# Samples' attention over the cached keys and values: steps of four tiles in place of two, and a fifth tile place

## The chip, the cores and the metric

The kernel runs on one core of one Trainium2 chip. The metric is device time in microseconds (us), the median of several runs. A core has five engines: TensorE (PE, matmuls; its weight loads are shown apart as PEld), VectorE (DVE), ScalarE (ACT), GpSimd (POOL) and SyncE (SP, which here only issues DMAs). Each takes its own instructions in order and waits on semaphores for the others. DMAs are issued by SP and POOL.

## What is computed

One layer of a decoder for two groups of tokens that share the weights: a prompt of 512 tokens, and 8 samples of 8 tokens each (64 in all). The layer is a mixer (two recurrences over one combined input projection), a cross-attention over 256 memory entries, and a gated feed-forward part, each between two norms and with a residual. All of it is float32. The change is in the cross-attention:

```python
qx = (u @ w_xq).reshape(bsz, length, 4, 256)
sc = einsum('blhd,bmhd->bhlm', qx, mem_k) * 256 ** -0.5
pr = softmax(sc, axis=-1)
o = einsum('bhlm,bmhd->blhd', pr, mem_v).reshape(bsz, length, 1024) @ w_xo
x = x + _rms(o) * g_post_x
```

For the prompt, `mem_k` and `mem_v` are computed in the kernel from `mem_prompt` with the weights `w_mem_k` and `w_mem_v`. For the samples they are inputs, `cache_mem_k` and `cache_mem_v`, of 8 samples x 256 entries x 4 heads x 256 values each, 8.4 MB a piece.

## The kernel before, in words

Activations lie transposed, channels on the 128 partitions and tokens along the free axis, prompt and samples side by side (576 columns, cut into halves of 256 and 320 or of 288). A float32 product with a weight is made of three faster ones: weight and activation are each split into a rounded high part and a low remainder, and PE does high by high, high by low and low by high (L202, L203, L205 in `gemm`; L795 to L797 for the memory's values). `split_w` (L175 to L187) loads a weight of 512 KB into one of two buffers called raw with a DMA on SP (L175), casts it on ACT to the high part whi (L180) and subtracts on DVE, or half on DVE and half on POOL, for the low part wlo (L187). whi and wlo have three buffers each. The weight's raw buffer is free when the low part is made, and its whi and wlo when PE has used them.

The instructions are written down in one order, and a scheduler with a timeline of its own then decides how the five engines' instructions interleave; `tc.issue_after` ties an instruction behind another one.

The attention of the prompt runs over the heads h = 3, 2, 1, 0 (the loop ahead of `attn_values(*last)`): query projection (`xq`, tile ps_xq), the memory's keys of the head (`mem_key`, ps_mk), transposes of the probabilities and attention times values of the head before (`attn_values`, ps_pt and ps_ov), scores and softmax (`attn_scores`, ps_at), the memory's values of the head (`mem_value`, ps_v). Behind the loop comes the output projection (`xo`, ps_xo), first for the tokens 0 to 287.

The attention of the samples is strewn into this as generators. `attn_samples_k(hb)` and `attn_samples_v(hb)` do scores with softmax, and probabilities times values, for the four samples 4 hb to 4 hb + 3. Both call `pick` (from L1395 on), which takes per sample two tiles of 128 x 1024 float32 (512 KB) out of the cache. `cached` (L1384 to L1389) loads such a tile with a DMA on SP (L1388) into the next of the places in `kv`, in turn: three in the slot s5 (the tiles called kva) and one in a pool of its own (kvb). For every tile PE does four matmuls of 32 columns (L1401), one for each head, into the 32 output partitions of that head; they are full float32 and show as two instructions each. When both samples of a pair are done, DVE takes from each head's rows those that belong to the sample (L1409, L1411). The pairs use two PSUM banks in turn (B0, B1). The softmax of the four samples and two transposes (ps_pts, L1427) end `attn_samples_k`; two transposes (ps_ots, L1436) and the split for the output projection end `attn_samples_v`.

The generators yield after the first sample of each pair and between the pairs, so that each takes four steps of two tiles: 16 steps in all. `sample_step(m)` takes the next step and ties it behind the instruction m. Steps are taken behind the first `xq` of a head, inside `mem_key`, inside `attn_scores` and behind `mem_value`; the last generator's four are taken in the loop of `xo` at j = 0, 1, 3 and 5. The order is: scores of the second four samples beside head 2, scores of the first four beside head 1, values of the second four beside head 0, values of the first four beside `xo`.

Ahead of all this, in the output projection of the mixer (ps_o, `out1` and `out2`), `presplit` (L1165 to L1183) prepares weights of later stages: it loads one on POOL's queue (tile prel, L1181), casts it on ACT (preh, L1174), subtracts on DVE (L1175) and writes the low part to DRAM on POOL's queue (pre, L1176). SP loads the memory's input (memraw, L1198) there, and further weights for ACT to cast (wmh, L191).

Of the kernel before, what the change touches and what calls it, by code (L numbers as in the profile page):

```python
# [11 lines left out]
F32 = mybir.dt.float32  # L12
# [7 lines left out]
P = 128  # L20
# [95 lines left out]
def build(nc, tc, ctx, I, O):  # L116
# [14 lines left out]
    def SL(slot, name, dt=F32, shape=(P, KT, T)):  # L131

        return big.tile(list(shape), dt, name=name, tag="s%d" % slot, bufs=1)


    def GP(name="g"):
        return pg.tile([P, 512], F32, name=name, tag="g")
# [17 lines left out]
    def C32(k):  # L155
        a, b = _c32[k]
        return c32[:, a:b] if b <= NLONG else c32e[:, a - NLONG:b - NLONG]
# [14 lines left out]
    def split_w(src, n=1024, cut=CUT, acc=False, pool=None, to=None, raw=None):  # L172
        if raw is None:
            raw = wp.tile([P, 1024], F32, name="raw", tag="raw", bufs=2)
        loads.append(S.dma_start(raw[:, :n], src))  # L175
        if to:
            split(*to, raw[:, :n])
            return to
        hi, lo = [(pool or wp).tile([P, 1024], F32R, name=k, tag=k, bufs=NWX if pool else 3) for k in ("whi", "wlo")]
        casts.append(A.copy(hi[:, :n], raw[:, :n]))  # L180
        for e, a, b in ((V, 0, cut), (G, cut, n)):
            if b > a and e is G and acc:

                A.activation(lo[:, a:b], hi[:, a:b].bitcast(F32), AF.Copy, scale=-1.0)  # L184
                G.dma_start(lo[:, a:b], src[:, a:b], accum_op=ALU.add)  # L185
            elif b > a:
                e.tensor_tensor(lo[:, a:b], raw[:, a:b], hi[:, a:b].bitcast(F32), op=ALU.subtract)  # L187
        return hi, lo

    def split(hi, lo, src, eng=None, cast=None):  # L190
        c = (cast or A.copy)(hi, src)  # L191
        (eng or V).tensor_tensor(lo, src, hi.bitcast(F32), op=ALU.subtract)  # L192
        return c

    def gemm(ps, units, xh, xl, t0, n, k0=0, k1=None, order=None, late=0):


        tiles = [(hi[:, j * P:(j + 1) * P], lo[:, j * P:(j + 1) * P]) for hi, lo, nk in units for j in range(nk)]
        order = order or range(len(tiles))
        for i, k in list(enumerate(order))[k0:k1]:  # L200
            (wh, wl), ah, al = tiles[k], xh(k, t0, n), xl(k, t0, n)
            mm(ps, wh, ah, start=i == 0, stop=False)  # L202
            mm(ps, wh, al, start=False, stop=False)  # L203
            for c in range(late) if i == late - 1 else [i] if i >= late else ():
                m = mm(ps, tiles[order[c]][1], xh(order[c], t0, n), start=False, stop=c == len(tiles) - 1)  # L205
        return m
# [503 lines left out]
    for g in range(2):  # L710
# [13 lines left out]
        for h in range(8):  # L724
            k, j = h % 2, (8 * g + h) // 2
# [434 lines left out]
    at = st.enter_context(tc.tile_pool(name="attn", bufs=1, reuse_waits="tile"))  # L1160
# [60 lines left out]
    def out2(j, i):  # L1221
        return gemm2([(*weights(("o", j), I["wout"][j, 1], cut=1024), KT)], act(mixm_h), act(mixm_l), o2_evac(j), "ps_o2", [i])
# [30 lines left out]
    m = out2(7, 0)  # L1253
    with tc.issue_after(m.ins):
        rc = rstd_cols([ssq], HCHUNKS[1], "po1", alloc=B0)
    m = out2(6, 0)
# [9 lines left out]
    s5 = SL(5, "kva", F32, (P, 4608))  # L1266
# [3 lines left out]
    def sample_step(m):  # L1270

        with tc.issue_after(m.ins):
            next(steps, None)

    def mem_act(i):
        return lambda k, t0, n: memh[:, i, k, t0:t0 + n]

    def mem_key(h, ws=None):

        mk = at.tile([P, 2, 2, 256], F32R, name="mk", tag="mk", bufs=1)  # L1280
        mo = at.tile([P, 2, 256], F32, name="mko", tag="mo", bufs=2)
        for kk in range(2):
            ps = GP("ps_mk")[:, 0:256]
            m = gemm(ps, [(*(ws[kk] if ws else split_w(I["wmk"][2 * h + kk])), KT)], mem_act(0), mem_act(1), 0, 256)
            if kk == 0:
                sample_step(m)
            V.tensor_tensor(mo[:, kk, :], ps, rmem_b, op=ALU.mult)
            split(mk[:, 0, kk, :], mk[:, 1, kk, :], mo[:, kk, :], None if ws else G)
        S.dma_start(O["mk"][:, 2 * h:2 * h + 2, :], mo)
        return (mk, m) if ws else mk  # L1290

    def mem_value(h, ws=None):

        mv = at.tile([P, 2, 2, 256], F32R, name="mv", tag="mv", bufs=1)
        mo = at.tile([P, 2, 256], F32, name="mvo", tag="mo", bufs=2)

        def ev(_, ps):
            for c in range(2):
                A.activation(mo[:, c, :], ps[:, c * 256:(c + 1) * 256], AF.Copy, scale=rmem[0][:, c:c + 1])
            split(mv[:, 0], mv[:, 1], mo)  # L1300
            S.dma_start(O["mv"][:, :, h * 256:(h + 1) * 256], mo)

        m = gemm_tok(I["wmv"][h], mem_act(0), mem_act(1), CHUNKS[:2], ev, units=ws)
        return mv, m
# [6 lines left out]
    def xq(j, i):  # L1311
        return gemm2([(*weights(("xq", j), I["wxq"][j], cut=1024 if i else CUT), KT)], act(u2h), act(u2l), q_evac(j), "ps_xq", [i])
# [66 lines left out]

    kxs = ExitStack()  # L1380
    kx = kxs.enter_context(tc.tile_pool(name="kx", bufs=1, side="right", reuse_waits="tile"))
    kv = [s5[:, 1024 * i:1024 * i + 1024] for i in range(3)] + [kx.tile([P, 1024], F32, name="kvb")]
    turn = [0]

    def cached(src):
        t_ = kv[turn[0] % len(kv)].rearrange("p (h m) -> p h m", h=4)
        turn[0] += 1
        S.dma_start(t_, src)  # L1388
        return t_  # L1389

    def pick(dst, hb, src, lhs, name):

        for pair in range(2):
            ps = (B0, B1)[pair](name)
            for b2 in range(2):  # L1395
                b = 2 * pair + b2
                o = ps[:, 256 * b2:256 * b2 + 256]
                for d in range(2):
                    t_ = cached(src[4 * hb + b, :, d])
                    for h in range(4):  # L1400
                        mm(o[32 * h:32 * h + 32, :], lhs(h, d), t_[:, h, :], start=d == 0, stop=d == 1,  # L1401
                           skip_group_check=True)
                if not b2:
                    yield
            for b2 in range(2):
                b = 2 * pair + b2
                o = ps[:, 256 * b2:256 * b2 + 256]
                if b == 0:
                    V.tensor_scalar(dst, o, C32("bmask")[:, 0:1], None, op0=ALU.mult)  # L1409
                else:  # L1410
                    V.scalar_tensor_tensor(dst, o, C32("bmask")[:, b:b + 1], dst, op0=ALU.mult, op1=ALU.add)  # L1411
            if not pair:
                yield

    def attn_samples_k(hb):
        pr, pt = s5[:, 3072 + 256 * hb:3328 + 256 * hb], s5[:, 3584 + 256 * hb:3840 + 256 * hb]
        yield from pick(pr, hb, I["kc"], lambda h, d: qsm[:, 2 * h + d, 32 * hb:32 * hb + 32], "ps_sa")
        mx = at.tile([P, 1], F32, name="mxs")
        sm = at.tile([P, 1], F32, name="sms")
        V.reduce_max(mx, pr, axis=AX.X)  # L1420
        V.tensor_scalar(mx, mx, -1.0 / 16.0, None, op0=ALU.mult)
        A.activation(pr, pr, AF.Exp, scale=1.0 / 16.0, bias=mx, accum_out=sm)
        V.reciprocal(sm, sm)
        V.tensor_scalar(pr, pr, sm, None, op0=ALU.mult)
        pst = (B0, B1)[hb]("ps_pts")
        for m in range(2):
            TE.transpose(pst[:, m * P:(m + 1) * P], pr[:, m * P:(m + 1) * P], ident)  # L1427
        A.copy(pt, pst[:, 0:256])
# [14 lines left out]
    mk, m = mem_key(3, wm[:2])  # L1443
    with tc.issue_after(m.ins):
        rc = rstd_cols([ssq], HCHUNKS[0], "po0", alloc=B0)
    mv, m = mem_value(3, wm[2:])
# [10 lines left out]
    m = xq(4, 1)  # L1457
    with tc.issue_after(m.ins):
        rc2[1] = rstd_cols([ssq2], HCHUNKS[1], "p21", alloc=B1)
    m = xq(5, 1)  # L1460
    with tc.issue_after(m.ins):
        rstd_rows(rc2[1][:, 2:3], HCHUNKS[1][2:], rb2, B1)
    m = xq(6, 1)
# [7 lines left out]
    for h in range(3, -1, -1):  # L1471

        sample_step(xq(2 * h + 1, 0))
        xq(2 * h, 0)
        if last:
            mk = mem_key(h)
            attn_values(*last)
        pr = attn_scores(h, mk)
        if last:
            mv, m = mem_value(h)  # L1480
            sample_step(m)
        last = h, pr, mv
        steps = attn_samples_k(h - 2) if h > 1 else attn_samples_v(h)
    attn_values(*last)
    st.close()


    bx = ctx.enter_context(tc.tile_pool(name="bx", bufs=1, reuse_waits="tile"))
# [31 lines left out]
    for j in range(8):  # L1520
        step = xo(j, 0, wx if 3 < j < 7 else None)
        if j < 3:

            step(0, KT - 2)
            with tc.issue_after(ends[-1].ins) if j else ExitStack():
                ends.append(step(KT - 2, KT)[0])
        else:
            ends.append(step(0, KT)[0])

        if j < 2:  # L1530
            next(steps, None)
        elif j in (3, 5):
            sample_step(ends[-1])
    kxs.close()
    u3l = SL(5, "u3l", F32R)
# [821 lines left out]
```

## Time and profile before

| | us |
|---|---|
| Median of 3 runs | 1092.81 |
| Lowest and highest run | 1091.64, 1092.93 |
| The profiled execution, whole time | 1092.94 |
| Its span, from the first to the last instruction | 1091.2 |
| PE busy from 543 to 668 us (the samples' attention) | 124.61 of 125.00 |
| PE busy from 395 to 543 us (output projection of the mixer, first queries) | 147.36 of 148.00 |
| PE busy from 668 us to the end (rest of `xo`, feed-forward part) | 415.97 of 423.20 |

The profile comes from one execution. A row of its timeline gives start, length, engine, line, operation, the tile written and the tiles read, the form (partitions, elements) and how many equal instructions follow each other; in brackets stands how long the engine was idle before it and what ended the idleness. PE's matmuls overlap, so the distance from one start to the next is what a matmul costs, not its length. A row of DMA issue on SP (SPq) tells when the DMA was handed over, not when its data landed. The chain that ended last is followed back from the last instruction: at each step to what released it, or to the instruction before it on its engine. A row of windows gives a stretch, its length, the busy time (and instructions) of PE, PEld, DVE, ACT and POOL, the granted clock, the busy share of the 16 DMA engines and the GB/s that they moved.

### The profile page before, as it was taken

The numbers are of one execution on the slowest core, as the hardware profiler recorded it, in microseconds if no ns is written. First come the engines' busy times: TensorE is split into PE (matmuls) and PEld (weight loads), VectorE is DVE, ScalarE is ACT, GpSimd is POOL, SyncE is SP. The second block draws the span as 40 slices with busy tenths as digits, with TensorE's granted clock in tenths as the row PEclk, the third lists the DMA queues.
The fourth block names the chain that finished last, engine by engine and source line by source line (L and its number), as shares of the span: only waits on it lengthen the run. The fifth ranks groups of instructions, "written<-read, shape, count | busy, mean of one in ns | idle before, by whom it ended". The sixth has DMA issues, their size and how long they took to land.

```text
span 1091.2 us, 20715 instructions
## 1 busy us (share of the span) xinstructions
PE 1079.0 (99%) x8124; PEld 1021.6 (94%) x8124; DVE 753.5 (69%) x1507; ACT 611.5 (56%) x1098; POOL 225.2 (21%) x305
## 2 busy tenths in 40 slices
PE   9999999999999999999999999999999999999997
PEld 8999887778999999999988879999999999999997
DVE  6896785758877775569644546666567887787555
ACT  7867632355654555566544545646567566656653
POOL 1332643313213111000244301100011121111000
PEclk9999999999999999999999999999999999999999
DMA  6785634435655348653468765644486687577532
GB/s 206 176 160 127 163 110 172 164 91 172 191 149 154 102 148 287 202 201 114 143 216 278 274 232 175 224 150 100 118 182 146 149 203 170 115 190 183 128 130 88
DMA packets 58966, 182.29 MB, mean 167 GB/s; under 512 B 6604, under 2 KB 11852, under 8 KB 58356
## 3 DMA queue, kind: packets, MB, share of 16 engines
q1 hardware_dynamic: 42740, 138.06, 38.7%
q0 software_dynamic: 15552, 41.95, 19.7%
q8 instruction: 64, 1.05, 0.4%
q10 hardware_dynamic: 576, 0.95, 0.3%
q14 instruction: 34, 0.28, 0.1%
HBM read 160.28 MB, written 20.65 MB: 166 GB/s over the span
## 4 chain that ended last, share of the span: by engine, by line
PE 80%; DVE 6%; DMA 5%; ACT 5%; issue 3%; POOL 1%; SPq 0%; DVEq 0%; ACTq 0%; POOLq 0%
PE ps_in L203 4%; PE ps_in L202 4%; PE ps_in L205 4%; PE ps_v L815 3%; PE ps_g L1849 3%; PE ps_g L1850 3%; PE ps_u L1850 3%; PE ps_u L1851 3%; PE ps_g L1851 3%; PE ps_u L1849 3%; PE ps_dn L1849 2%; PE ps_dn L1850 2%; PE ps_dn L202 2%; PE ps_dn L203 2%; PE ps_dn L1851 2%
## 5 line engine op out<-in xcount | busy, mean ns | idle before, releaser
L202 PE MATMUL ps_in<-uh,whi 128*128 128x320 f32 (+1 forms) x544 | 162.9, 300 | 0.8 <-DVE cb L451 0.5
L205 PE MATMUL ps_in<-uh,wlo 128*128 128x320 f32 (+1 forms) x544 | 162.1, 298 | 0.3 <-DMA wlo<-win 0.3
L203 PE MATMUL ps_in<-ul,whi 128*128 128x320 f32 (+1 forms) x544 | 161.7, 297 | 0.0
L180 ACT CAST whi<-raw 128x1024 fp32r<-128x1024 f32 (+1 forms) x104 | 105.3, 1013 | 97.6 <-PE ps_in L203 25.8
L187 DVE TENSOR_TENSOR wlo<-raw,whi 128x512 fp32r<-128x512 f32 (+1 forms) x96 | 97.2, 1015 | 69.2 <-ACT whi L180 68.3
L202 PEld LDWEIGHTS ps_in<-uh,whi 128*128 128x128 f32 x544 | 102.7, 189 | 3.9 <-issue 1.7
L205 PEld LDWEIGHTS ps_in<-uh,wlo 128*128 128x128 f32 x544 | 102.2, 188 | 1.4 <-DMA wlo<-win 0.5
L203 PEld LDWEIGHTS ps_in<-ul,whi 128*128 128x128 f32 x544 | 102.3, 188 | 0.6
L185 POOL DMA_DIRECT2D wlo<-win x32 | 27.8, 869 | 80.4 <-ACT wlo L184 72.3
L1850 PE MATMUL ps_g<-b,whi 128*128 128x288 f32 x144 | 42.5, 295 | 0.0
L1850 PE MATMUL ps_u<-b,whi 128*128 128x288 f32 x144 | 42.4, 295 | 0.0
L1849 PE MATMUL ps_g<-b,whi 128*128 128x288 f32 x144 | 42.4, 294 | 0.0
L1849 PE MATMUL ps_u<-b,whi 128*128 128x288 f32 x144 | 42.2, 294 | 0.0
L1822 ACT CAST whi<-rawx 128x1024 fp32r<-128x1024 f32 (+1 forms) x26 | 25.6, 985 | 27.2 <-PE ps_dn L1850 13.7
L192 DVE TENSOR_TENSOR wlo<-sw,whi 128x1024 fp32r<-128x1024 f32 (+1 forms) x26 | 29.6, 1140 | 15.7 <-ACT whi L191 15.6
L202 PE MATMUL ps_xo<-qh,whi 128*128 128x288 f32 x128 | 38.7, 304 | 0.2 <-ACT whi L180 0.2
L205 PE MATMUL ps_o<-mixm_h,wlo 128*128 128x256 f32 (+1 forms) x128 | 38.0, 297 | 0.6 <-DVE wlo L187 0.6
L205 PE MATMUL ps_o<-mixs_h,wlo 128*128 128x320 f32 (+1 forms) x128 | 37.7, 295 | 0.0
L203 PE MATMUL ps_xo<-ql,whi 128*128 128x288 f32 x128 | 37.7, 296 | 0.0
L203 PE MATMUL ps_o<-mixs_l,whi 128*128 128x320 f32 (+1 forms) x128 | 37.7, 294 | 0.0
L202 PE MATMUL ps_xq<-u2h,whi 128*128 128x320 f32 (+1 forms) x128 | 37.7, 298 | 0.0
L203 PE MATMUL ps_o<-mixm_l,whi 128*128 128x256 f32 (+1 forms) x128 | 37.7, 294 | 0.0
(765 smaller groups left out, 3836.0 us busy)
## 6 DMA issues: line engine op xcount, KB each, us to landing
raw<-win SPq DMA_DIRECT2D x35, 512.0 KB, 4.0
raw<-wout SPq DMA_DIRECT2D x17, 512.0 KB, 3.6
raw<-wxq SPq DMA_DIRECT2D x13, 512.0 KB, 3.6
raw<-wgate SPq DMA_DIRECT2D x13, 512.0 KB, 3.6
raw<-wup SPq DMA_DIRECT2D x13, 512.0 KB, 5.0
wlo<-win POOLq DMA_DIRECT2D x24, 256.0 KB, 5.0
kva<-kc SPq DMA_DIRECT2D x12, 512.0 KB, 5.7
kva<-vc SPq DMA_DIRECT2D x12, 512.0 KB, 5.7
```

Of the source, the lines that this page charges most:

```text
L180: casts.append(A.copy(hi[:, :n], raw[:, :n]))
L185: G.dma_start(lo[:, a:b], src[:, a:b], accum_op=ALU.add)
L187: e.tensor_tensor(lo[:, a:b], raw[:, a:b], hi[:, a:b].bitcast(F32), op=ALU.subtract)
L192: (eng or V).tensor_tensor(lo, src, hi.bitcast(F32), op=ALU.subtract)
L202: mm(ps, wh, ah, start=i == 0, stop=False)
L203: mm(ps, wh, al, start=False, stop=False)
L205: m = mm(ps, tiles[order[c]][1], xh(order[c], t0, n), start=False, stop=c == len(tiles) - 1)
L815: mm(ps, a, b, skip_group_check=True, **kw)
L1822: A.copy(s.h3[:, s.all], s.r2[:, s.all])
L1849: mm(ps, wh, b[0][k], start=start and k == 0, stop=False, skip_group_check=True)
L1850: mm(ps, wh, b[1][k], start=False, stop=False, skip_group_check=True)
L1851: m = mm(ps, wl, b[0][k], start=False, stop=k == nk - 1, skip_group_check=True)
```

## The change

- `pick` no longer yields after the first sample of a pair. A generator has two steps of four tiles, and there are eight steps.
- Steps are taken behind the first `xq` of a head and inside `attn_scores`; those of `mem_key` and behind `mem_value` are gone. In the loop of `xo` they are taken at j = 1 and j = 4.
- `kv` gets a fifth place, a tile of 4 KB per partition (kvc) in the attention's pool `at`. When that pool is closed after the loop over the heads, the place is taken off again, and the last eight tiles go round the four.

The number of tiles, matmuls and DVE operations stays. Lines behind the first edit move up by two to four: the samples' matmuls of L1401 stand at L1399.

```diff
@@ mem_key
             m = gemm(ps, [...], mem_act(0), mem_act(1), 0, 256)
-            if kk == 0:
-                sample_step(m)
             V.tensor_tensor(mo[:, kk, :], ps, rmem_b, op=ALU.mult)
@@ places of the cached tiles
-    kv = [s5[:, 1024 * i:1024 * i + 1024] for i in range(3)] + [kx.tile([P, 1024], F32, name="kvb")]
+    kv = [s5[:, 1024 * i:1024 * i + 1024] for i in range(3)] + [kx.tile([P, 1024], F32, name="kvb"), at.tile([P, 1024], F32, name="kvc")]
@@ pick
                     for h in range(4):
                         mm(o[32 * h:32 * h + 32, :], lhs(h, d), t_[:, h, :], start=d == 0, stop=d == 1,
                            skip_group_check=True)
-                if not b2:
-                    yield
@@ loop over the heads
         if last:
             mv, m = mem_value(h)
-            sample_step(m)
         last = h, pr, mv
         steps = attn_samples_k(h - 2) if h > 1 else attn_samples_v(h)
     attn_values(*last)
     st.close()
+    kv.pop()
@@ loop of xo
-        if j < 2:
+        if j == 1:
             next(steps, None)
-        elif j in (3, 5):
+        elif j == 4:
             sample_step(ends[-1])
```

## The prediction

> **What bounds the kernel now.** I read the page's busy times first, then the chain that ended last, then what TensorE (PE) waits for (in total, times, longest), and last the timeline of the stage that the change touches.
>
> ```profile
> span 1091.2 us, 20715 instructions
> PE 1079.0 (99%) x8124; PEld 1021.6 (94%) x8124; DVE 753.5 (69%) x1507; ACT 611.5 (56%) x1098; POOL 225.2 (21%) x305
> PE 80%; DVE 6%; DMA 5%; ACT 5%; issue 3%; POOL 1%; SPq 0%; DVEq 0%; ACTq 0%; POOLq 0%
> ```
>
> ```profile
> PE ps_o L205 <- DVE wlo L187: 0.6, 1, 0.6
> ...
> PE ps_xo L202 <- ACT whi L180: 0.2, 1, 0.2
> PE ps_v L797 <- POOL wlo L187: 0.2, 1, 0.2
> ```
>
> PE is busy in 99% of the span, and behind its start no wait of it is longer than 0.6 us. So the kernel gets faster only where PE gets less to do or where one of these few waits goes; it gets slower where a new wait of PE appears. The other engines matter through what they deliver late.
>
> The change touches the samples' attention. Its matmuls are 32 columns wide and strewn into a stream of 128-wide ones. Here are one place of 16 such instructions and the one place of 32 (start, length, engine, line, operation, tiles, form, count), and then the first and the last of the 19 places that the timeline has:
>
> ```profile
> 553.86 0.28 PE L203 MATMUL ps_mk<-memhl,whi 128*128 128x256 f32 x1
> 553.98 0.28 PE L205 MATMUL ps_mk<-memhl,wlo 128*128 128x256 f32 x1
> 554.19 0.64 PE L1401 MATMUL ps_sa<-kva,qsm 128*32 128x256 f32 x8
> 554.64 0.61 PE L1401 MATMUL ps_sa<-kvb,qsm 128*32 128x256 f32 x8
> 555.19 0.39 PE L202 MATMUL ps_mk<-memhl,whi 128*128 128x256 f32 x1
> 555.41 0.28 PE L203 MATMUL ps_mk<-memhl,whi 128*128 128x256 f32 x1
> ```
>
> ```profile
> 611.05 1.50 PE L1401 MATMUL ps_os<-kva 128*32 128x256 f32 x24
> 612.37 0.61 PE L1401 MATMUL ps_os<-kvb,kva 128*32 128x256 f32 x8
> 612.91 0.39 PE L205 MATMUL ps_mk<-memhl,wlo 128*128 128x256 f32 x1
> ```
>
> ```profile
> 543.77 1.06 PE L1401 MATMUL ps_sa<-kva,qsm 128*32 128x256 f32 x12
> ...
> 658.01 0.64 PE L1401 MATMUL ps_os<-kva 128*32 128x256 f32 x8
> ```
>
> The 128-wide stream advances by 0.12 us (553.86 to 553.98). The 16 instructions take 555.19 - 554.19 = 1.00, the 32 take 612.91 - 611.05 = 1.86. So 16 more cost 0.86, and 0.14 is paid once per place. Going in takes 554.19 - 553.98 = 0.21 instead of 0.12, and the first advance behind it 555.41 - 555.19 = 0.22 instead of 0.12. A place costs 0.09 + 0.14 + 0.10 = **0.33 us** beside its work, on the engine that sets the end.
>
> **The change, part by part.** *Fewer places.* Sixteen steps of two tiles become eight of four. The order of the changed program's PE instructions does not have eight places, because the scheduler still cuts some: its runs are 6, 10, 16, 4 and 12 (parted by two transposes alone), 16, 16, 16, 1, 14, 1 and 16 program matmuls, each two instructions in the trace. That is 12 places for 19, with the same 128 matmuls; a tile cut in two counts twice, and by that count both orders visit 35 tiles. 7 x 0.33 = **2.33 us less** (7 x 0.333). The vector work of a step (mask and add, softmax, transposes back) keeps its number and moves with it, off PE.
>
> *A wait that is left behind.* The third wait of the second fence stands here:
>
> ```profile
> 589.47 0.28 PE L796 MATMUL ps_v<-whi,memhl 128*128 128x256 f32 x1
> 589.93 0.38 PE L797 MATMUL ps_v<-wlo,memhl 128*128 128x256 f32 x1 [0.18 <-POOL wlo L187]
> 590.15 0.28 PE L795 MATMUL ps_v<-whi,memhl 128*128 128x256 f32 x1
> ```
>
> 589.93 - 589.47 is 0.46 and 590.15 - 589.93 is 0.22, against 0.12 each: 0.44 us for 0.18 of idleness, so a restart costs 0.26. It waits for the second value weight of head 1. In the changed order only 12 of the 48 value matmuls, which need the first weight alone, stand ahead of the attention-times-values matmuls, both sets of scores and the merged step; all that need the second come behind these. I take the 0.44 as saved; bounds 0 and 0.44. The 0.2 us of ps_xo stays: its weight still waits for the buffer of an earlier one.
>
> *The fifth place.* It adds no load, but lets one of the 32 be issued early. In the changed order that load stands on SP's queue right behind the second load of memraw, so at about 402 us. That is where the chain that ended last leaves PE for 59 us:
>
> ```profile
> 401.40 6.88 DMA memraw<-memT
> ...
> 416.69 8.88 DMA pre<-prel
> ...
> 436.25 5.52 DMA prel<-wup
> ...
> 445.32 5.04 DMA raw<-wout
> ...
> 452.72 5.04 DMA raw<-wout
> ...
> 460.20 0.41 PE ps_o L205
> ```
>
> The place itself is free by then: what lay there was last read by the transposes of L936, done by 390. The row of the windows below (us; busy time of five engines; clock, DMA share, GB/s) tells how full the DMA engines are at that point.
>
> ```profile
> L936 PE MATMUL ps_ht<-c,num x32: 270/272/328, 287.6 to 389.7; 128*128 128x128 f32 x32
> ```
>
> ```profile
> 401.00:413.00 12.00, 12.00 (x94) 12.00 (x93) 6.65 (x10) 7.34 (x13) 2.23 (x4) 1.00 0.77 283
> ```
>
> ```profile
> kva<-kc SPq DMA_DIRECT2D x12, 512.0 KB, 5.7
> ```
>
> The chain of hops (weights read, halved, written back, then the next) ends in PE's longest wait, so what it loses PE loses. 512 KB are 0.52 MB; at 283 GB/s they take 1.85 us, the upper bound. From below: the changed order lets ACT cast one wout weight before a cast that waits for a DMA, which moves a wmk load ahead of the hop of 445.32; at best the whole wait goes, 0.6 and a restart of 0.26, 0.9 us. Bounds -0.9 and +1.85. I take **+0.3**, nearer the middle: memraw's own loads are ahead of the new one on SP, the hops behind it run on POOL's queue, and the engines have room (0.77).
>
> The Trainium skill ("DMA: Bandwidth & Descriptors", section "Queues, rings and completion order") says that each DMA engine takes turns, packet by packet, between the queues that have work. By that rule a load added to SP's queue takes nothing from POOL's hops as long as SP has other loads under way anyway; the 0.3 would be 0 and the time 1090.0. Nothing in this trace shows it by itself.
>
> *Loads that move on SP's queue.* SP issues in order, and a merged step frees its places later. Before (SP, then the value weight of 574.40 on ACT, POOL and PE, then all tile loads from issue to landing, then a window):
>
> ```profile
> 567.72 4.70 SPq L1388 DMA_DIRECT2D kva<-kc  x3
> ...
> 573.02 0.38 SPq L1388 DMA_DIRECT2D kvb<-kc  x1
> 573.46 0.55 SPq L1301 DMA_DIRECT2D o_mv<-mvo  x1
> 574.40 0.51 SPq L175 DMA_DIRECT2D raw<-wmv  x1
> ```
>
> ```profile
> 581.49 1.05 ACT L180 CAST whi<-raw 128x1024 fp32r<-128x1024 f32 x1 [1.31 <-DMA raw<-wmv]
> ```
>
> ```profile
> 582.62 1.80 POOL L187 TENSOR_TENSOR wlo<-raw,whi 128x512 fp32r<-128x512 f32 x1 [1.38 <-ACT whi L180]
> ```
>
> ```profile
> 587.06 0.36 PE L795 MATMUL ps_v<-whi,memhl 128*128 128x256 f32 x1
> ```
>
> ```profile
> DMA to landing us min/median/max: 3.7/6.3/8.1
> ```
>
> ```profile
> 575.00:584.00 9.00, 9.00 (x92) 7.58 (x91) 4.38 (x11) 4.05 (x8) 3.18 (x2) 1.00 1.02 378
> ```
>
> Tiles first. The merged step that follows the one near 567 needs three places which that one frees. Their loads leave at about 567.5, 568.0 and 568.4 (a tile every 0.45, as 554.19 to 554.64) and are used from about 575.8, 576.3 and 576.7. At the slowest landing, 568.4 + 8.1 = 576.5: no wait, barely.
>
> Then the value weight. Three tile loads stand ahead of it whose places come free one after the other in the merged step, the last at about 577.1, so it leaves 2.7 us later than at 574.40. Before, it landed at 581.4 (7.0 us), and POOL had its part of the low half ready at 584.42. PE needs that part eight advances and a slow one behind 587.06, at about 588.2. Slack 3.8, minus 2.7, minus the 2 x 0.33 that PE is earlier by then, leaves 0.4. I take **0**; at 8.1 us of landing it would be 0.7.
>
> The sum: -2.33 - 0.44 + 0.3 + 0 = -2.47. The profiled execution took 1092.94 (the span and 1.7 around it), 0.13 above the median of 1092.81. 1092.94 - 2.47 - 0.13 = **1090.3**. Behind the stage nothing gives it back: PE has no listed wait there, and what feeds it is released by its own progress.
>
> **The rivals.** *B, the early load eats the gain.* The chain takes the full 1.85 us and the wait of 589.93 stays: -2.33 + 1.85 = -0.48, 1092.3. For it: the chain has no slack at 460.20. Against: only its first hop is on SP's queue.
>
> *C, the chain gets shorter.* The wait of 460.20 goes and the load costs nothing: -2.33 - 0.44 - 0.9 = -3.67, 1089.1. For it: the hop of 445.32 is rid of a wmk load beside it. Against: that load then runs beside the hop of 436.25.
>
> *D, the value weight comes late, and the kernel is slower.* The load of 574.40 now has three tiles, itself and the 256 KB of o_mv to wait for, 2.36 MB. At the 378 GB/s of the last window these take 6.2 us, under the 7.0 that it had. But over longer stretches the stage moves less; of the 40 slices of this row it covers the 21st to the 25th, 216 to 175:
>
> ```profile
> GB/s 206 176 160 127 163 110 172 164 91 172 191 149 154 102 148 287 202 201 114 143 216 278 274 232 175 224 150 100 118 182 146 149 203 170 115 190 183 128 130 88
> ```
>
> At 175 they take 13.5 us, and PE waits 13.5 - 7.4 = 6.1 at the value matmuls: -2.47 + 6.1 = +3.6, 1096.4. It decides from 9.9 us of landing (7.4 + 2.5), below 238 GB/s. Against it: no tile load took over 8.1 us.
>
> **How the numbers follow.** My forecast has 0.58 and a range of its own of 1089.4 to 1091.2 (the 0.3 at -0.6, or at 0.7 with the 0.44 not saved); B 0.15; C 0.12; D 0.15. A measurement of this kernel tells some 0.2%, 2.2 us, from no change, so faster means below 1090.6. Three quarters of the forecast (0.44) and C lie there: 0.56. Slower is D and a hundredth of B, where more comes together: 0.16. The remaining 0.28 is the same. The range is 1088.9 to 1093.5: the forecast, B and C with the small costs at their bounds; D is left out.
>
> **What would show it.** Right: 12 places of 32-wide matmuls, each 0.33 us beside its work, and no wait of PE in the value matmuls of head 1. Wrong: a wait of PE on L187 ahead of those value matmuls, or on a tile's DMA, which is D; a wait of ps_o near 460 grown well past 0.6, which is B, or gone, which is C. If there are 12 places and the stage is no shorter, the price of a place was wrong.

## The result, and the profile after

The change made the kernel slower by a quarter of a per cent: 1094.93 us median of 22 runs (1091.84 to 1099.42) against 1092.13 us (1090.79 to 1093.46; also 22 runs) of the kernel before in the same comparison, ratio 1.0025, 95% interval 1.0017 to 1.0033. Forecast were 1090.3 and a range of 1088.9 to 1093.5. The profiled execution took 1093.79, 1.1 below the median, so it shows less of the loss than a usual run has; more on that below.

The page of the profile after, its first lines:

```profile
span 1092.0 us, 20715 instructions
...
PE 1077.5 (99%) x8124; PEld 1021.9 (94%) x8124; DVE 755.2 (69%) x1507; ACT 611.5 (56%) x1098; POOL 226.6 (21%) x305
```

PE has the same 8124 instructions and 1.5 us less busy time than before (1079.0), in a span that is 0.8 us longer. So PE got less to do, as meant, and waits more. What PE waits for (in total, times, longest), in the view of its waits:

```profile
PE ps_v L795 <- ACT whi L180: 2.0, 2, 1.2
...
PE ps_v L797 <- DVE wlo L187: 0.4, 2, 0.2
...
PE ps_xo L202 <- ACT whi L180: 0.2, 1, 0.2
PE ps_v L797 <- POOL wlo L187: 0.2, 1, 0.2
```

The first row is new: twice a value matmul waits for the high part of its weight. The wait of ps_o, 0.6 us before, is not listed. The two places, in PE's timeline:

```profile
587.27 0.39 PE L795 MATMUL ps_v<-whi,memhl 128*128 128x256 f32 x1 [1.18 <-ACT whi L180]
...
618.23 0.39 PE L795 MATMUL ps_v<-whi,memhl 128*128 128x256 f32 x1 [0.84 <-ACT whi L180]
```

587.27 is the first value matmul of head 1, 618.23 the first of head 0 that needs its second weight. The chain that ended last says where each comes from (start, length, what):

```profile
574.47 0.57 PE ps_sa L1399 x8
575.04 0.37 PE ps_pts L1423 x2
575.41 1.04 PE ps_sa L1399 x16
576.47 0.39 SPq L1386
576.95 9.14 DMA raw<-wmv
586.17 1.05 ACT whi L180
587.29 1.81 POOL wlo L187
589.14 0.39 PE ps_v L797
...
609.73 1.81 POOL wlo L187
611.56 5.47 DMA raw<-wmv
617.13 1.05 ACT whi L180
618.21 0.70 DVE wlo L187
618.95 0.39 PE ps_v L797
```

Read the first part upward from 576.95: the load of the value weight was handed over right behind a tile load on SP (L1386), and that one had waited for the merged step's matmuls (ps_sa) to free its place. This is the queue on SP that rival D named. The second part has no tile load in the chain itself: there a raw buffer came free late (POOL's low half, 609.73 + 1.81 = 611.54), and the load, cast and low half that follow are too late for head 0. What else was under way beside that load is looked at behind e4.

Now the length of the stage. Its ends in PE's timeline, the first 32-wide matmul and the first matmul of the feed-forward part, after (before it ran from 543.77, shown with the prediction):

```profile
543.72 1.06 PE L1399 MATMUL ps_sa<-kva,qsm 128*32 128x256 f32 x12
...
694.12 0.30 PE L202 MATMUL ps_g<-u3h,w 128*128 128x288 f32 x1
```

and the end of it before:

```profile
693.26 0.29 PE L202 MATMUL ps_g<-u3h,w 128*128 128x288 f32 x1
```

149.49 us before, 150.40 after: +0.91. Behind the stage nothing differs (397.90 us to the end of the span in both). In it PE idles for 2.86 us in six waits, 0.39 us in two before; with the prediction's 0.26 of a restart for each, that is 2.47 + 4 x 0.26 = 3.51 more. So the rest of the stage got 2.60 us shorter, by seven stretches (places of 32-wide matmuls): 0.37 each. The gain was there, and the waits took it and more.

### The profile page after: what moved, and what is told of

Same layout as the page of the kernel before. It is cut to its first block, busy times and chain, and to the rows that moved or that the text cites. A ratio compares the mean times of both kernels' runs of the same rounds, so it can differ in the third digit from the quotient of the medians.

```text
span 1092.0 us, 20715 instructions
## 1 busy us (share of the span) xinstructions
PE 1077.5 (99%) x8124; PEld 1021.9 (94%) x8124; DVE 755.2 (69%) x1507; ACT 611.5 (56%) x1098; POOL 226.6 (21%) x305
## 4 chain that ended last, share of the span: by engine, by line
PE 84%; DVE 5%; ACT 4%; DMA 3%; issue 2%; POOL 1%; SPq 0%; DVEq 0%; ACTq 0%; POOLq 0%
PE ps_in L203 4%; PE ps_in L202 4%; PE ps_in L205 4%; PE ps_v L815 3%; PE ps_o L205 3%; PE ps_o L203 3%; PE ps_g L1845 3%; PE ps_g L1846 3%; PE ps_o L202 3%; PE ps_g L1847 3%; PE ps_u L1847 3%; PE ps_u L1846 3%; PE ps_u L1845 3%; PE ps_dn L1845 2%; PE ps_dn L1846 2%
## 5 line engine op out<-in xcount | busy, mean ns | idle before, releaser
L180 ACT CAST whi<-raw 128x1024 fp32r<-128x1024 f32 (+1 forms) x104 | 105.1, 1013 | 107.1 <-PE ps_in L203 25.7
```

## The experiments

Stretches are counted in PE's order; "ahead" is how many of head 1's 48 value matmuls stand ahead of the first of its two sets of scores; "stage" and "idle" (PE's idle time in it) are from the first profile of each kernel. The ratio is to the kernel before, timed beside each group of runs (e, f, g; its medians are 1092.07 to 1092.23), with its 95% interval.

| | stretches | ahead | stage | idle | median us | ratio |
|---|---|---|---|---|---|---|
| before | 19 | 34 | 149.49 | 0.39 | 1092.1 | |
| the change | 12 | 12 | 150.40 | 2.86 | 1094.93 | 1.0025 (1.0017 to 1.0033) |
| e1, five places, short steps | 19 | 34 | 149.64 | 0.39 | 1091.83 | 0.9998 (0.9989 to 1.0007) |
| e2, four places, long steps | 13 | 31 | 149.03 | 1.30 | 1091.54 | 1.0000 (0.9991 to 1.0008) |
| e3, weights early on SP | 12 | 12 | 153.00 | 4.08 | 1093.05 | 1.0008 (0.9999 to 1.0018) |
| e4, weights on POOL's queue | 12 | 12 | 152.04 | 4.20 | 1094.57 | 1.0024 (1.0016 to 1.0033) |
| f2, values ahead of scores | 14 | 48 | 148.03 | 1.19 | 1091.34 | 0.9992 (0.9983 to 1.0001) |
| f3, long steps, own raw buffer | 13 | 37 | 147.03 | 0.34 | 1090.91 | 0.9984 (0.9975 to 0.9993) |
| f4, short steps, own raw buffer | 19 | 33 | 149.23 | 0.21 | 1091.81 | 0.9995 (0.9986 to 1.0004) |
| g1, f3 with two passes on POOL | 13 | 37 | 146.49 | 0.21 | 1089.73 | 0.9976 (0.9968 to 0.9985) |
| g2, f3 with four passes on POOL | 14 | 37 | 147.85 | 0.43 | 1090.46 | 0.9984 (0.9975 to 0.9993) |

### e1: the fifth place alone

```diff
 (the kernel before, with)
+    ... + [kx.tile([P, 1024], F32, name="kvb"), at.tile([P, 1024], F32, name="kvc")]
...
+    kv.pop()
```

> The kernel before with the fifth place alone (taken off again after the loop over the heads); the steps stay two tiles long and PE's order is that of before. Theory D (the loss of the change comes from the first value weight of head 1, queued on SP behind three tile loads): that weight has only one tile load of before's kind ahead of it here, so no wait of PE on L180 at the value matmuls; the time is at or a little below before's, 1091.2 to 1092.3 on a scale where before is 1092.1, lower if the early load of the fifth place lets the 0.6 us wait at 460 us go (rival C of the prediction, 0.9 us). Rival R1 (the fifth place costs: more tile loads under way at once slow the others): slower than before by 1 us or more, wide spread of the runs.

1091.83, no wait on L180, 19 stretches: the place by itself shows no cost and no gain (within the interval, some 1 us). R1, which had 1 us or more of cost, falls.

### e2: the long steps alone

```diff
 (the change, without)
-    ..., at.tile([P, 1024], F32, name="kvc")]
...
-    kv.pop()
```

> The change without the fifth place: steps of four tiles, four places. The first value weight of head 1 stands behind three tile loads on SP here too. Theory D: the wait of PE at head 1's value matmuls stays, 1 to 4 us, and with the 2.3 us of the fewer stretches gone the time is 1093 to 1096 where before is 1092.1. Rival R1 (the fifth place costs): the loss goes, 1089.5 to 1090.5. If the wait at 460 us is back in its profile, it was the fifth place's early load that took it away.

1091.54, neither as fast as R1 had it nor as slow as D had it. The wait at head 1's value matmuls stays (0.5 us on L180), the one on L180 at head 0 is gone. So the fifth place does have a part together with the long steps. Two things differ in the traces: with the place the scheduler puts 12 value matmuls of head 1 ahead of its scores and merged step, without it 31; and with the place three tile loads leave ahead of the second value weight of head 0, while without it they leave behind that weight. No run parts the two.

### e3 and e4: the value weights earlier, PE's order as in the change

```diff
 e3, attn_scores, heads 2 to 0
             if tp == 0:
+                ws = [split_w(I["wmv"][h][:, i, :]) for i in range(2)]
                 sample_step(m)
...
-            mv, m = mem_value(h)
+            mv, m = mem_value(h, ws)
```

```diff
 e4, split_w as called for the values
-        loads.append(S.dma_start(raw[:, :n], src))
+        loads.append(G.dma_start(raw[:, :n], src))
```

> The change, with the loads of both value weights of a head written down ahead of the merged step inside the scores; on SP the first value weight of head 1 then stands ahead of the three tile loads, PE's order is the same as in the change. Theory D: the wait on L180 at head 1's value matmuls goes (2.4 us in the profiled run of the change, more in slower runs), 1090 to 1091.5 where before is 1092.1; the spread of the runs shrinks from 7.6 us to some 3 us. Rival R2 (the longer stretches and the value matmuls pushed behind them are the cause, wherever the weight is queued): 1094.5 to 1095.5 as the change.

> The change, with the loads of the value weights of heads 2, 1 and 0 issued on POOL's queue, where nothing is queued ahead of them but POOL's own low halves; PE's order is the same as in the change. Theory D: the wait on L180 at head 1's value matmuls goes, 1090 to 1091.5 where before is 1092.1. Rival R2: 1094.5 to 1095.5 as the change. If the weight is issued early and still lands late (over 9 us), the transfers share the DMA engines and the queue is not the cause: then the wait stays at 1 us or more.

1093.05 and 1094.57: D alone is not enough. e4 lies in R2's range, e3 between the two, and the runs of e3 spread over 5.5 us instead of 3. At head 1 D was right, PE waits no more on L180 in e3 and 0.07 us in e4. But the wait at head 0 grew. PE's timeline of e3, then of e4:

```profile
619.16 0.39 PE L795 MATMUL ps_v<-whi,memhl 128*128 128x256 f32 x1 [2.48 <-ACT whi L180]
```

```profile
619.02 0.39 PE L795 MATMUL ps_v<-whi,memhl 128*128 128x256 f32 x1 [2.45 <-ACT whi L180]
```

What PE no longer waits for at head 1, it waits for at head 0: counted from the start of the stage, this matmul runs at 74.5 us in the change and at 75.6 and 76.1 here. So the second wait is not set by the first; it has a time of its own. Both kernels also have a wait that the change has not, 0.98 us at 595.13 in e3 and 0.83 at 614.90 in e4, each ended by DVE's work on ql, so they are not the change less one wait. In e4 the weights also landed late from another queue (8.5 us for the first of head 1, 8.0 for both of head 0).

The candidate was the 36 value matmuls pushed behind scores and step. The first value weight is in use up to the 36th of a head's 48 (4 of 8 k-blocks of each half, three matmuls each: 12, and 12 more behind the 24th). Only then is its whi buffer free for a later cast. That 36th matmul before, in PE's timeline:

```profile
597.14 0.28 PE L797 MATMUL ps_v<-wlo,memhl 128*128 128x256 f32 x1
```

and after, the first and the last of the 36 that stand behind the merged step:

```profile
597.36 0.28 PE L795 MATMUL ps_v<-whi,memhl 128*128 128x256 f32 x1
...
601.49 0.28 PE L797 MATMUL ps_v<-wlo,memhl 128*128 128x256 f32 x1
```

The 24th of these is the 36th of all, at about 597.36 + 23 x 0.118 = 600.1, 2.9 us later than before. ACT's next weight cast before, after and in e2:

```profile
598.10 1.04 ACT L180 CAST whi<-raw 128x1024 fp32r<-128x1024 f32 x1
```

```profile
600.36 0.56 ACT L1351 ACTIVATE pr<-ps_at,mx,scol 128x256 f32<-128x256 f32 x1
...
600.90 2.00 ACT L180 CAST whi<-raw 128x1024 fp32r<-128x1024 f32 x2
```

```profile
599.11 1.05 ACT L180 CAST whi<-raw 128x1024 fp32r<-128x1024 f32 x1 [1.80 <-POOL pr L1355]
```

In the change the cast is 2.8 us later than before, queued behind the last softmax row of the scores; in e2, whose stage begins 0.95 us earlier than that of before, it is 2.0 later in the stage. In the change the raw buffer that it empties takes head 0's second key weight, that one's buffer the second value weight (the second part of the chain above): it leaves at 611.56 instead of 609.86. This is theory T2 of the next runs.

The late release is not the whole of the second wait. The loads that SP hands over around that weight, and the 4 us from the weight's own hand-over, in the change and then before:

```profile
606.86 0.80 SPq L1386 DMA_DIRECT2D kva<-vc  x2
607.76 0.38 SPq L1386 DMA_DIRECT2D kvb<-vc  x1
611.56 0.33 SPq L175 DMA_DIRECT2D raw<-wmv  x1
...
611.56:615.56 4.00, 4.00 (x38) 4.00 (x37) 1.36 (x3) 1.56 (x3) 2.54 (x2) 1.00 0.98 373
```

```profile
609.86 0.33 SPq L175 DMA_DIRECT2D raw<-wmv  x1
...
613.46 1.39 SPq L1388 DMA_DIRECT2D kva<-vc  x3
...
609.86:613.86 4.00, 4.00 (x52) 2.94 (x51) 1.12 (x2) 1.40 (x2) 1.79 (x1) 1.00 0.43 135
```

In the change three tile loads, freed by a merged step, leave ahead of the weight; the DMA engines are busy for 0.98 of the time, and the weight takes 5.5 us. Before, the tile loads leave behind it, the share is 0.43, and it takes 3.6. From its hand-over to its cast 5.6 to 7.0 us pass in the five profiles of the change, 3.7 and 4.1 in the two of before. In f1, the second profile of the change, the weight leaves 65.8 us behind the start of the stage, as early as before (65.7 and 66.1), takes 7.0, and PE waits longest, 1.75 us. In e2 the 36th matmul runs 56.05 us behind the start, as late as in the change (54.84 to 56.68), but the tile loads leave behind the weight, it takes 4.9, and PE does not wait on L180. So the late release and the tile loads beside the weight both go into this wait, and no run parts them.

### f1: the change a second time

> The change, unaltered, profiled a second time. If its loss is waits of PE whose length hangs on when loads land, the same two places (the first value matmul of head 1, a value matmul of head 0) wait again, by other amounts, together 1 to 6 us, and nothing else in the stage does. If the 0.6 us wait at 460 us in the profile of before was chance of that execution, this one may have it or not; the instruction order there says nothing. A loss that sits elsewhere (starts, feed-forward part) would speak against both theories.

1092.48, stage 149.80: no wait on L180 at head 1 (the weight landed in 7.6 us, 9.1 in the first profile), 1.75 us at head 0. So only one of the two places waits for the high part of a weight here, and longer than in the first profile. The wait at 460 us is absent again.

### f2: the value matmuls ahead of the scores

```diff
+        if last:
+            mv, m = mem_value(h)
         pr = attn_scores(h, mk)
-        if last:
-            mv, m = mem_value(h)
```

> The change (four-tile steps, five places) with the value products of a head written down ahead of its scores, so that PE's order has all 48 of them ahead of the second scores and the merged step, in 14 stretches of 32-wide matmuls. Theory T2 (the second wait, at head 0, comes from value matmuls that were moved behind scores and step and so release the weight buffers late): no wait on L180 at head 0's value matmuls; with the first wait down too (the weight has the released tile loads only ahead of it) the time is 1090 to 1091.2 where before is 1092.1. Rival R3 (loads come in bursts of four and land late whatever the order): the waits stay, 1093.5 to 1095.

1091.34, just above the forecast, and no wait on L180 at either head's value matmuls, with the long steps and the five places of the change. So both waits hang on the order of the value matmuls, as T2 had it, and R3's forecast falls. Its premise stays: three of the four value weights of heads 1 and 0 still take 7.0 to 8.3 us to land, but all four leave 2.6 to 5.1 us earlier in the stage than in the first profile of the change. The 1.19 us of idleness that it has are elsewhere (0.3 and 0.1 for cached tiles, 0.2 to 0.3 each in `xo`, where the kernel before has 0.2 once).

### f3 and f4: the 4 KB as a raw buffer for the first value weight

```diff
 gemm_tok; f3: in e2, f4: in the kernel before
-        units = units or [split_w(src[:, i, :], cut=cut) for i in range(2)]
+        units = units or [split_w(src[:, i, :], cut=cut, raw=at.tile([P, 1024], F32, name="rawv", tag="rawv", bufs=1) if i == 0 else None)
+                          for i in range(2)]
```

> The change without the fifth place; its 4 KB are a raw buffer of their own for the first value weight of each head, which so leaves a head earlier. 13 stretches. If late weights are the whole loss: no wait of PE over 0.3 us from 543 to 693 us, 1089.6 to 1090.6 where before is 1092.1. Rival R3 (bursts): the second value weight still lands late, waits of 1 us and more, 1092 or above.

> The kernel before, steps of two tiles in 19 stretches, with a raw buffer of its own for the first value weight of each head. If the price of a stretch is 0.31 to 0.33 us, this is 1.9 to 2.0 us slower than the same buffer under the longer steps; by itself it can only take away the 0.44 us at 590 us: 1091.5 to 1092.1 where before is 1092.1. If it is as fast as the kernel with the longer steps and the buffer, the stretches' price is wrong.

f3 took 1090.91, a little above its forecast, and beats both kernels; f4 took 1091.81. The same buffer under 13 and 19 stretches: the stage is 147.03 against 149.23, 2.20 us for six stretches, close to the 1.9 to 2.0 that were expected, while the medians differ by 0.9 only, with some 1 us of uncertainty on each ratio. All that PE waits for in f3 from 543 to 693 us (in total, times, longest):

```profile
PE ps_xo L202 <- ACT whi L180: 0.2, 1, 0.2
```

Too short for this view, 0.13 us are left at 590.03. With the weights in time the stage with the long steps is shorter.

### g1 and g2: a wait set by hand, which did not come about

```diff
 gemm_tok, in f3, head 0; n = 2 (g1), n = 4 (g2)
+        lo = units[1][1][:, cut:1024]
+        for _ in range(n):
+            G.tensor_scalar(lo, lo.bitcast(F32), 1.0, None, op0=ALU.mult)
```

> The kernel with four-tile steps and a raw buffer for the first value weight (f3), with two more passes of POOL (times 1.0, in place) over POOL's half of the low part of head 0's second value weight, so that PE's wait there is set by hand: some 0.5 to 2 us. Theory C1 (a wait of PE costs its length and 0.26 us, and beyond about 2 us now and then a drop of the granted clock behind it, 4 us at 0.55 to 0.60 as in the profile of e3, 1.8 us more): f3's 1090.9 and the wait, 1091.5 to 1093, clocks of the runs as in f3. Rival C2 (the waits' length varies with the landing of loads and the clock has no part in it): the same time.

> As g1 with four passes: a wait some 2 to 4 us longer than g1's, 3 to 6 us. C1: the time grows by the longer wait and by up to 1.8 us more, the mean granted clock of the runs falls from f3's 0.997 by 0.001 to 0.003, and the profile shows a window of 4 us at 0.5 to 0.6 behind the wait. C2: the time grows by the longer wait alone and the clock stays.

Neither has a wait there: the scheduler counted the passes in and moved attention-times-values and others ahead of the matmuls that need this weight. So they say nothing on C1 and C2. But g1, with two useless passes, is the fastest of all by its median, 1089.73 (its interval overlaps those of f3 and g2): its stage of 146.49 has one wait of 0.21 us in it. That is 3.0 us less than before.

### g3: the kernel before a second time

> The kernel before, unaltered, profiled a second time. The wait of 0.6 us at 460 us was missing in all nine other profiles, one of them with the same order of instructions up to there. If it was chance of one execution, it is missing here, and the start differs from the first profile's by up to 2 us. If it is back, the kernel before has it as a rule, and its going in the others is a gain of theirs.

1092.14; the wait at 460 us is missing, stage 149.36. So the kernel before does not have it as a rule.

### h1 to h3: the change three times more

> The change, unaltered, profiled a third time. C1 (waits, and behind a long one a drop of the granted clock): in a run of 1095 or more a window of some 4 us at 0.5 to 0.6 inside the stage, and waits at the value weights of 2 us or more. C2 (waits alone): waits that add up to the whole excess over 1090, clock 1.00 through the stage.

> The change, unaltered, profiled a fourth time. Expected as in h1: C1, a window of some 4 us at 0.5 to 0.6 inside the stage if the run is one of 1095 or more; C2, longer waits at the value weights and a clock of 1.00.

> The change, unaltered, profiled a fifth time. Expected as in h1: C1, a window of some 4 us at 0.5 to 0.6 inside the stage if the run is one of 1095 or more; C2, longer waits at the value weights and a clock of 1.00.

1093.66, 1094.19 and 1094.31; none was a run of 1095 or more. So what the slowest runs look like, which C1 and C2 were to tell, was not seen. The waits on L180, head 1 and head 0: 0.92 and 1.03, 1.51 and 0.95, 0.47 and 1.66 us; stages of 150.34, 150.85 and 150.54, clock 1.00 in the stage. And h3 has the wait at 460 us, in PE's timeline:

```profile
460.49 0.42 PE L205 MATMUL ps_o<-mixm_h,wlo 128*128 128x320 f32 x1 [0.54 <-DVE wlo L187]
```

So it comes and goes with the execution, with and without the change.

## Why the prediction was wrong

*Fewer places: right.* 12 stretches, as counted, at 0.37 us each by the profile after (0.33 forecast); f3 against f4 gives 2.20 for six, also 0.37, before their waits are taken off.

Two other steps failed. With the small waits behind them and 0.26 for each restart, PE lost some 1.9 us at head 1 and 2.0 at head 0, on the mean of the five profiles of the change; the sum had nothing for either.

*"I take the 0.44 as saved": the first step that failed, by what it left out.* The wait of POOL's low half at 589.93 did go. But the 36 value matmuls were put behind scores and merged step for nothing, since what they need is ready by then. What they hold was left out: the buffers of the value weights. In the first profile their release 2.9 us later put ACT's next cast, two raw buffers and the second value weight of head 0 late. Left out as well was what that weight meets when it leaves: the tile loads of a merged step, beside which its landing took some 2 us longer. PE waited 0.84 to 1.75 us on L180 at head 0 in five profiles. f2 (all 48 ahead) and f3 (37 ahead, and a buffer more) have no such wait; e3 and e4 (12 ahead, weights earlier) have 2.5 us of it.

*"I take 0" for the value weight of head 1: the second step that failed, the mechanism right and the size off.* It left at 576.95, 2.55 us later than before (2.7 forecast). The sum took a landing of 7.0 and gave 0.7 us at 8.1; it landed in 7.6 to 9.5, and PE waited 0 to 1.51 us at head 1 in the five profiles. The 8.1 us, the slowest tile load in the profile before, was no bound: three tile loads and the weight now leave within 1.7 us. Rival D was the right place at the wrong price, 6.1.

*The fifth place: 0.3 of cost on the chain, measured as none, for a reason that was not given.* The early load does slow POOL's hops. The 10 us from the first hop's hand-over, with the share of the queues (q0 is POOL's, q1 SP's) and the hops' landing, in the change and then in e2, which has no such load:

```profile
q1 hardware_dynamic: 699, 1.92, 56.6%
q0 software_dynamic: 386, 1.44, 36.2%
...
prel<-wxo POOLq DMA_DIRECT2D x2, 512.0 KB, 8.7
...
prel<-wgate POOLq DMA_DIRECT2D x1, 512.0 KB, 11.5
```

```profile
q1 hardware_dynamic: 656, 1.58, 44.6%
q0 software_dynamic: 432, 1.57, 43.3%
...
prel<-wxo POOLq DMA_DIRECT2D x2, 512.0 KB, 6.5
prel<-wgate POOLq DMA_DIRECT2D x1, 512.0 KB, 8.8
```

The hops land 2.2 to 2.7 us later than in e2, and 1.4 to 2.0 later than in g3 (7.3 and 9.5 there): about the upper bound of 1.85. This is no chance of one execution: the hop of wgate takes 10.7 to 11.7 us in all 13 profiles with 512 KB more at this point (the fifth place, or the raw buffer of f3, f4, g1 and g2), and 8.8 to 9.5 in the three without. The rule of the Trainium skill ("DMA: Bandwidth & Descriptors", section "Queues, rings and completion order"), as the prediction applied it, had POOL's hops unharmed; the trace disagrees with that reading, q0 moved 1.44 MB instead of 1.57. The reading had a condition, that SP has other loads under way anyway, and no run shows whether it held all the time, so the taking of turns itself is not refuted.

Yet PE did not pay. From the second load of memraw to the start of the stage 141.3 us pass in 14 of the 16 profiles, with the load and without; in the other two, the first of before and h3, it is 1.0 more, and these are the two with the wait at 460 us. So the chain has slack in most executions, and "what it loses PE loses" did not hold. One profile had been taken for the rule, and rivals B and C both stood on it. The fifth place did matter, in the stage: e2, without it, has a ratio of 1.0000, the change 1.0025. With it the scheduler puts 19 fewer value matmuls ahead; the prediction had read that order and priced only what it removed.

*How much of the loss is explained.* The five profiles of the change have stages of 149.80 to 150.85, mean 150.39; the two of before 149.49 and 149.36: 0.96 us. The medians differ by 2.8, but in the one comparison that timed the change many times. The four other profiled executions of the change, in groups f and h, took 1092.48 to 1094.31, which is 0.3 to 1.1 us above the kernel before beside them. Part of the rest goes with the clock: the 22 runs of the change have a mean granted clock of 0.9962, the 84 runs of before beside the groups e to h 0.9974 (for the 22 beside the change it is not known), which is 0.0012 x 1092 = 1.3 us; within the 22 runs the four above 1096 have 0.993 or 0.994, and clock and time are correlated with -0.69. Even with these 1.3 us, half a microsecond stays unexplained. What a fall of the clock behind a wait looks like shows in the profile of e3, a run of 1096.28, in its windows behind the wait of 619.16:

```profile
619.00:621.00 2.00, 1.62 (x9) 1.19 (x9) 1.86 (x4) 1.49 (x4) 1.82 (x2) 1.00 0.00 0
621.00:623.00 2.00, 2.00 (x10) 1.94 (x10) 0.36 (x1) 0.00 (x0) 0.68 (x1) 0.60 0.90 188
623.00:625.00 2.00, 2.00 (x6) 1.53 (x5) 0.00 (x0) 0.00 (x0) 0.00 (x0) 0.55 0.60 209
625.00:627.00 2.00, 2.00 (x14) 1.77 (x13) 0.70 (x2) 1.22 (x3) 0.00 (x0) 1.00 0.00 0
```

The clock column (third from the end) is at 0.60 and 0.55 for 4 us: 0.8 + 0.9 = 1.7 us lost beside the wait itself. No profile of the change shows such a drop in the stage; none was of a run above 1095. A drop of the same size at 80 to 84 us in f1 (0.61 and 0.54) did not cost as much: the stage begins at 543.01 there, earlier than in the four other profiles of the change. And f4, which has no wait over 0.21 us in the stage, has that drop too. So a low mean clock is no sign of waits in this stage by itself; that the slower runs lose their time as e3 does is possible by their clocks, and stays open.

## What to carry to other kernels

When matmuls are moved back, price what they hold as well as what they need: find the last reader of each weight buffer in the new order, follow the next cast, load and use from there, a round or two on, and see which other loads are then under way. A wait seen in one profile at the end of a DMA chain may be that execution's alone; a second profile of the same kernel tells it from a rule before a term of the sum is built on it. Where a longer step saves switches, try a spare buffer on the weight that then queues behind its loads (f3), not on the step itself.

## What had not been expected of the hardware

Behind a wait of PE of 2.48 us, with another 0.2 soon after, the granted clock was 0.50 for 3.4 us (e3, 621.4 to 624.8); behind one of 2.45 us in e4 it did not fall. In f1 and f4 it fell in the same way at 80.4 us, with no idle time of PE above 0.41 us in the 8 us ahead, and in e1 at 26.9, 1.7 us behind a wait of 1.19. The Trainium skill ("TensorE: Matmul & The Clock Gate", section "What's actually happening") has the clock halved after an idle window of about 3.4 us; the idle time here was shorter, so a wait under that figure is no safe one by these traces, and what sets off the drop stays open.

The landing of one and the same load differed from execution to execution: 7.6 to 9.5 us for the 512 KB of head 1's first value weight in five profiles of the change. A slack of 0.4 us worked out from one profile is within that spread.
